# q's opening in six pieces of x, matmul passes of 320, 256 and 288 columns, and each product's last chunk finished tile by tile

## The chip, the cores and the metric

The kernel runs on one core of a Trainium2 chip. The metric is the device time of one execution in microseconds (us), as the median of several runs. Times inside an execution come from one profiled execution, counted from the start of its span.

## The reference

One layer of a decoder is computed in float32 for 256 prompt rows and 32 sample rows (8 sequences of 4), so T = 288 rows of D = 2048. Cut to what matters here:

```
h = rms_norm(x, g_pre);  z = h @ w_in            # -> q | k | v | u | v_g, 1024 columns each
A = block-sparse attention(q, k, v, paged cache) # 8 heads of 128, rotary on q and k
B = gelu(u) * spatial_gating(layer_norm(gelu(v_g)))
mix = (sigmoid(h @ Wg_a) * (A @ Wa) + sigmoid(h @ Wg_b) * (B @ Wb)) @ w_o
x = x + rms_norm(mix)
x = x + rms_norm(SwiGLU(rms_norm(x)))            # FFN_HIDDEN = 5632
x = x + (p @ w_ple) * sigmoid(rms_norm(x) @ w_ple_gate)
```

## The kernel before

Activations lie transposed, features on the 128 partitions and the T rows along the free dimension; `x` is 16 slabs of 128 features (`KD = 16`). Each large product is a call of `product(w, c0, ks, ...)`, which makes 256 output columns as two PSUM tiles (t = 0 and 1) of 128 columns each. It walks the contraction in chunks of four slabs. For a chunk it loads 512 KB of weights on SyncE's queue (tile `wr`, four buffers), ScalarE rounds them to the high part (`wh`, L224), VectorE takes the rest (`wl`, L225). For each slab and tile TensorE then makes three passes, called a triplet below:

```
nc.tensor.matmul(accs[t], wh[:, i, c], x[:, :T + wide], start=k == 0, stop=False)               # L228
nc.tensor.matmul(accs[t][:, wide:T], wh[:, i, c], x[:, T + wide:], start=False, stop=False)     # L229
late["mm"] = nc.tensor.matmul(accs[t][:, :T], wl[:, i, c], x[:, :T], start=False, stop=k == n - 1)  # L230
```

`x` holds the high part of the activations in columns 0 to 287 and the low part in 288 to 575. With `wide=0` the passes have 288, 288 and 288 columns. With `wide=32`, which only the product with `w_ffn_out` (tile `f`) used, they have 320, 256 and 288: the first pass also takes 32 columns of the low part, into 32 more columns of PSUM. At the product's end ScalarE copies these out (`rest`, L234) and VectorE adds them back (L235), before `done` reads the tile.

The tiles of a product come from PSUM pools: up to the end of the attention `acc` has three banks, `aux` three and `long` two; after it `acc` has six. There is one order of instructions for each engine, set by a scheduler at build time; `tc.issue_after` ties a step behind another in that order.

q has four products of 256 columns. In the opening two of them (`q2`) go together: for each of four pieces of x (four slabs, 576 KB) come `h_parts` (L189 on ScalarE, L190 on VectorE: high and low part of x times its gain), one chunk of either product, the load of the next piece and the squares for the norm `r0`. The other two products follow, each product's result goes through `rope`, then k, v and the rest, with the pages of the cache (`kt`, `vt`, 512 KB each, three buffers of four pages) loaded and multiplied in between (`page_load`, L560, on SyncE's queue too). Constants (`cst`, `kcst`) come by GpSimd's queue, `cm` by ScalarE's. Ten warm-up matmuls (`wake`) run while the first loads are on their way.

The last stage multiplies with `w_ple_gate` (tile `pg`); `pg_done` makes two output tiles of each product and writes both in one transfer.

Of the kernel before, what the change touches and what calls it, by code (L numbers as in the profile page):

```python
# [41 lines left out]
QUADS = NPG // 4  # L42
WAKE, WR, BIG, PT, AUX, PB, LEAD, EG, LE, N1, N2, REST = 10, 4, 3, 1, 3, 2, 6, 2, 4, 20, 38, 325.0

# [64 lines left out]
def tile_hybrid_step(ctx: ExitStack, tc: tile.TileContext, a: dict, o: list):  # L109
# [25 lines left out]

    def x_load(c):
        nc.sync.dma_start(xs[c], a["x"][:, c * XK:c * XK + XK])
# [4 lines left out]
    x_load(0)  # L142
    cst = perm.tile([128, 128], F32, name="cst")
    nc.gpsimd.dma_start(cst, a["c_perm"][:, :128])
    ident = cst
# [8 lines left out]
    kcst = p_kv.tile([128, C_PERM - 128], F32, name="kcst")  # L154
    nc.gpsimd.dma_start(kcst, a["c_perm"][:, 128:])

# [28 lines left out]

    def h_parts(c):
        for i in range(XK):
            k = c * XK + i
            nc.scalar.activation(hh[:, k], xs[c][:, i], AF.Copy, scale=g_pre[:, k:k + 1])  # L189
            nc.vector.scalar_tensor_tensor(hl[:, k], xs[c][:, i], g_pre[:, k:k + 1], hh[:, k], op0=ALU.mult, op1=ALU.subtract)  # L190

# [8 lines left out]
    def r0_of():  # L200
# [5 lines left out]
        rstd_of(r0, r0p, p_x0.tile([128, T], F32, name="r0t"))  # L206


    def product(w, c0, ks, part, done, name, of="acc", wide=0, hold=()):


        accs = [bank([128, T + wide], f"{name}{t}", of) for t in range(2)]
        n = len(ks)
        for k0 in range(0, n, 4):
            m = min(4, n - k0)
            raw = perm.tile([128, 4, GC], F32, name="wr", bufs=WR)
            r0 = ks[k0] * 128
            nc.sync.dma_start(raw[:, :m], w[r0:r0 + m * 128, c0:c0 + GC].rearrange("(k p) c -> p k c", p=128))
# [28 lines left out]

    def q_gen(g, of="acc"):
        yield from product(w_in, g * GC, K16, hpart, lambda x: rope(qT[:, 2 * g:2 * g + 2], x), "q", of)
# [12 lines left out]
    p_a, end_a = pool("p_a", "right")  # L262
    cm = p_a.tile([128, C_MIX], F32, name="cm")
    nc.scalar.dma_start(cm, a["c_mix"])

# [506 lines left out]

    for q in q2 + [q_gen(2), q_gen(3)]:
        drain(q)
# [187 lines left out]
    for half in range(2):  # L962
# [41 lines left out]
        for g in range(8):  # L1004
            if half and g == 6:
                le_weights(range(LE, 8))
            drain(product(w_fo, g * GC, ks, lambda k: dhl[:, k], lambda x, g=g: fo_done(x, g), "f", wide=32))

# [5 lines left out]
    def pg_done(x, g):  # L1014
        for t in range(2):
            m = 2 * g + t
            gt = p_f.tile([128, T], F32, name="pgt", tag="fs", bufs=4)
            nc.vector.tensor_tensor(gt, x[t], r3, ALU.mult)
            nc.scalar.activation(gt, gt, AF.Sigmoid)
            nc.vector.tensor_tensor(gt, gt, le[:, m], ALU.mult)  # L1020
            nc.vector.tensor_tensor(x1[:, m], x1[:, m], gt, ALU.add)
        nc.sync.dma_start(y_o[:, 2 * g:2 * g + 2], x1[:, 2 * g:2 * g + 2])

# [57 lines left out]
```

## Time and profile before

| | us |
|---|---|
| median of 3 runs | 1820.64 (1820.21 to 1822.02) |
| the profiled execution | 1820.68 |
| its span, first to last instruction | 1818.9 |
| outside the span | 1.8 |
| TensorE busy | 1798.5 (99% of the span) |
| VectorE busy | 951.9 (52%) |
| ScalarE busy | 769.2 (42%) |

The profiled execution stands 0.04 us from the median, so its times can be set against it as they are. A busy share of TensorE is no measure of its pace: matmuls overlap, and a row's duration is longer than the distance from one start to the next. The pace of a stretch is its length over the number of matmuls that start in it.

### The profile page before, as it was taken

Reading aid. Unit: us, or ns where it says so; the run is one execution under the profiler, and the core shown is the slowest. Engines: PE = TensorE matmul, PEld = TensorE weight load, DVE = VectorE, ACT = ScalarE, POOL = GpSimd, SP = SyncE. Lnnn points to the kernel's source line nnn. Section 1 sums busy time; section 2 is a strip of 40 time slices with the busy share of each in tenths; the row PEclk is TensorE's granted clock in tenths of the full one; section 3 lists DMA queues with packets and bytes.
Section 4 is the critical chain, followed back from the end, with each engine's and each line's share of the span. In section 5 each row is a group of like instructions: output and inputs, shape, how many; then the busy total and the mean of one; then the engine's idle time right before and its main releaser. Section 6 shows DMA issues by size and latency. Waiting matters only on the chain.

```text
span 1818.9 us, 38387 instructions
## 1 busy us (share of the span) xinstructions
PE 1798.5 (99%) x15818; PEld 1752.1 (96%) x15818; DVE 951.9 (52%) x1363; ACT 769.2 (42%) x1081; POOL 90.6 (5%) x169
## 2 busy tenths in 40 slices
PE   7999999999999999999999999999999999999998
PEld 7999899999999989999999999999999999999998
DVE  6654447544344346544854555434455554444774
ACT  5334465444333344445533333333333333444642
POOL 1010112000000000011000000000000000011000
PEclk9999999999999999999999999999999999999999
DMA  9589999999999995555555555455555555546363
GB/s 345 163 280 367 323 360 337 365 350 359 352 345 368 358 321 201 170 164 161 152 169 166 163 167 169 157 168 165 172 165 172 163 164 170 165 158 195 122 196 112
DMA packets 309136, 414.81 MB, mean 228 GB/s; under 512 B 13120, under 2 KB 273344, under 8 KB 308832
## 3 DMA queue, kind: packets, MB, share of 16 engines
q1 hardware_dynamic: 307728, 409.16, 67.0%
q8 instruction: 124, 2.03, 0.5%
q0 software_dynamic: 944, 2.79, 0.4%
q10 hardware_dynamic: 288, 0.41, 0.1%
q14 instruction: 52, 0.43, 0.1%
HBM read 407.45 MB, written 4.85 MB: 227 GB/s over the span
## 4 chain that ended last, share of the span: by engine, by line
PE 94%; DVE 3%; DMA 1%; SPq 1%; issue 1%; ACT 1%; DVEq 0%; ACTq 0%
PE f L228 6%; PE f L230 5%; PE fg L228 5%; PE fg L230 5%; PE fg L229 5%; PE fa L230 5%; PE fa L228 5%; PE fa L229 5%; PE f L229 5%; PE values L696 3%; PE scores L598 3%; PE gb L228 2%; PE ga L228 2%; PE gb L230 2%; PE o L228 2%; PE o L230 2%
## 5 line engine op out<-in xcount | busy, mean ns | idle before, releaser
L225 DVE TENSOR_TENSOR wl<-wr,wh 128x1024 fp32r<-128x1024 f32 x512 | 618.8, 1209 | 708.2 <-ACT wh L224 704.4
L224 ACT CAST wh<-wr 128x1024 fp32r<-128x1024 f32 x512 | 530.9, 1038 | 881.0 <-PE f L229 140.4
L228 PE MATMUL f<-dhl,wh 128*128 128x320 f32 x704 | 217.1, 308 | 0.0
L229 PE MATMUL fg<-zhl,wh 128*128 128x288 f32 x704 | 208.2, 296 | 0.0
L230 PE MATMUL fa<-zhl,wl 128*128 128x288 f32 x704 | 206.8, 295 | 1.2 <-DVE wl L225 1.2
L229 PE MATMUL fa<-zhl,wh 128*128 128x288 f32 x704 | 207.9, 296 | 0.0
L228 PE MATMUL fg<-zhl,wh 128*128 128x288 f32 x704 | 207.3, 295 | 0.2 <-ACT wh L224 0.2
L230 PE MATMUL fg<-zhl,wl 128*128 128x288 f32 x704 | 207.0, 295 | 0.0
L230 PE MATMUL f<-dhl,wl 128*128 128x288 f32 x704 | 207.0, 294 | 0.0
L228 PE MATMUL fa<-zhl,wh 128*128 128x288 f32 x704 | 206.3, 296 | 0.1
L229 PE MATMUL f<-dhl,wh 128*128 128x256 f32 x704 | 196.6, 279 | 0.0
L230 PEld LDWEIGHTS fa<-zhl,wl 128*128 128x128 f32 x704 | 133.3, 189 | 1.4 <-DVE wl L225 1.4
L230 PEld LDWEIGHTS fg<-zhl,wl 128*128 128x128 f32 x704 | 133.3, 190 | 0.0
L229 PEld LDWEIGHTS f<-dhl,wh 128*128 128x128 f32 x704 | 132.4, 188 | 0.0
L228 PEld LDWEIGHTS fg<-zhl,wh 128*128 128x128 f32 x704 | 132.1, 188 | 0.4 <-ACT wh L224 0.4
L229 PEld LDWEIGHTS fa<-zhl,wh 128*128 128x128 f32 x704 | 132.4, 188 | 0.1
L229 PEld LDWEIGHTS fg<-zhl,wh 128*128 128x128 f32 x704 | 132.3, 188 | 0.0
L228 PEld LDWEIGHTS fa<-zhl,wh 128*128 128x128 f32 x704 | 131.6, 188 | 0.7 <-ACT zhl L937 0.4
L230 PEld LDWEIGHTS f<-dhl,wl 128*128 128x128 f32 x704 | 132.2, 188 | 0.0
L228 PEld LDWEIGHTS f<-dhl,wh 128*128 128x128 f32 x704 | 132.0, 188 | 0.0
L228 PE MATMUL gb<-hhl,wh 128*128 128x288 f32 x256 | 76.7, 300 | 0.0
L228 PE MATMUL ga<-hhl,wh 128*128 128x288 f32 x256 | 76.5, 299 | 0.0
(327 smaller groups left out, 3740.6 us busy)
## 6 DMA issues: line engine op xcount, KB each, us to landing
wr<-in_w_ffn_in SPq DMA_DIRECT2D x176, 512.0 KB, 3.7
kt<-in_cache_k SPq DMA_DIRECT2D x128, 512.0 KB, 7.7
vt<-in_cache_v SPq DMA_DIRECT2D x128, 512.0 KB, 6.6
wr<-in_w_in SPq DMA_DIRECT2D x80, 512.0 KB, 7.2
wr<-in_w_ffn_out SPq DMA_DIRECT2D x80, 512.0 KB, 3.4
wr<-in_w_gate SPq DMA_DIRECT2D x64, 512.0 KB, 7.4
wr<-in_w_o SPq DMA_DIRECT2D x32, 512.0 KB, 3.5
wr<-in_w_ple_gate SPq DMA_DIRECT2D x32, 512.0 KB, 3.5
```

The lines of the kernel that those rows point to most:

```text
L224: nc.scalar.copy(wh[:, :m], raw[:, :m])
L225: nc.vector.tensor_tensor(wl[:, :m], raw[:, :m], wh[:, :m], ALU.subtract)
L228: nc.tensor.matmul(accs[t], wh[:, i, c], x[:, :T + wide], start=k == 0, stop=False)
L229: nc.tensor.matmul(accs[t][:, wide:T], wh[:, i, c], x[:, T + wide:], start=False, stop=False)
L230: late["mm"] = nc.tensor.matmul(accs[t][:, :T], wl[:, i, c], x[:, :T], start=False, stop=k == n - 1)
L598: i = nc.tensor.matmul(sp[b][32 * g:32 * g + 32, 4 * n:4 * n + 4], Q[:, h2, g, dq], kt[:, :, c:c + 32], start=h2 == 1 and dq == 0, stop=h2 ...
L696: i = nc.tensor.matmul(oa[b][32 * g:32 * g + 8], w[:, n, 32 * g + 8 * part:32 * g + 8 * part + 8], v[:, :, g], start=first and part == 3, ...
```

## The change

It does five things. All products get `wide=32`. q's opening takes three products together instead of two (tiles from `acc`, `long` and `aux`), and takes x in six pieces of 1, 1, 2, 4, 4 and 4 slabs, with weight chunks of the same size (small ones in tiles `w1` and `w2`). The constants and `cm` go to SyncE's queue behind certain weight loads, and the first twelve cache pages are each tied behind a weight load, from the tenth on. In a product's last chunk all slabs of tile 0 come before those of tile 1. The very last output tile is finished in two halves of 144 columns, and the last product writes each of its output tiles by itself. The warm-up has eight matmuls instead of ten.

```diff
+    pieces = [(0, 1), (1, 2), (2, 4)] + [(k, k + XK) for k in range(XK, KD, XK)]
+    def x_load(k0, k1):
+        (nc.scalar if k0 == 1 else nc.sync).dma_start(xs[k0 // XK][:, k0 % XK:k0 % XK + k1 - k0], a["x"][:, k0:k1])
...
-    def product(w, c0, ks, part, done, name, of="acc", wide=0, hold=()):
+    def product(w, c0, ks, part, done, name, of="acc", wide=32, cuts=None, hold=()):
         accs = [bank([128, T + wide], f"{name}{t}", of) for t in range(2)]
         n = len(ks)
-        for k0 in range(0, n, 4):
-            m = min(4, n - k0)
-            raw = perm.tile([128, 4, GC], F32, name="wr", bufs=WR)
+        for k0, k1 in cuts or [(k, min(k + 4, n)) for k in range(0, n, 4)]:
+            m = k1 - k0
+            if cuts and m < 4:
+                raw = p_x0.tile([128, m, GC], F32, name=f"w{m}", bufs=6 // m)
+            else:
+                raw = perm.tile([128, 4, GC], F32, name="wr", bufs=WR)
...
-            for i, t in [(i, t) for i in range(m) for t in range(2)] if m == 4 else [(i, t) for t in range(2) for i in range(m)]:
+            steps = [(i, t) for i in range(m) for t in range(2)]
+            for i, t in sorted(steps, key=lambda s: s[1]) if k1 == n else steps:
...
-    q2 = [q_gen(0), q_gen(1, "long")]
-    for c in range(KD // XK):
-        h_parts(c)
-        for q in q2:
+    q3 = [q_gen(g, of, pieces) for g, of in enumerate(("acc", "long", "aux"))]
+    for i, (k0, k1) in enumerate(pieces):
+        h_parts(k0, k1)
+        for q in q3:
+            if k1 == KD and q is q3[2]:
+                squares(k1 // XK - 1)
+                with tc.issue_after(late["mm"].ins):
+                    r0_of()
             next(q)
-        if c + 1 < KD // XK:
-            x_load(c + 1)
-        squares(c)
-    r0_of()
+        if 1 < i + 1 < len(pieces):
+            x_load(*pieces[i + 1])
+        if k1 % XK == 0 and k1 < KD:
+            squares(k1 // XK - 1)
+    with tc.issue_after(loads[11].ins):
+        nc.sync.dma_start(cst, a["c_perm"][:, :128])
+        nc.sync.dma_start(kcst, a["c_perm"][:, 128:])
...
+            if len(issued) < FIRST:
+                st.enter_context(tc.issue_after(loads[9 + len(issued)].ins))
...
+            for c in (slice(0, T // 2), slice(T // 2, T)) if m == KD - 1 else (slice(0, T),):
+                nc.vector.tensor_tensor(gt[:, c], x[t][:, c], r3[:, c], ALU.mult)
+                nc.scalar.activation(gt[:, c], gt[:, c], AF.Sigmoid)
+                nc.vector.tensor_tensor(gt[:, c], gt[:, c], le[:, m, c], ALU.mult)
+                nc.vector.tensor_tensor(x1[:, m, c], x1[:, m, c], gt[:, c], ALU.add)
```

What the scheduler makes of it is seen at three places. The first is the start of SyncE's queue, where all weights, x and pages are issued (`x_76` to `x_79` are x's four tiles of four slabs). Before:

```order
L137 DMA x_76<-in_x 128x1152
L218 DMA wr<-in_w_in 128x4x256 x2
L137 DMA x_77<-in_x 128x1152
L218 DMA wr<-in_w_in 128x4x256 x2
L137 DMA x_78<-in_x 128x1152
L137 DMA x_79<-in_x 128x1152
L559 TENSOR_LOAD pt_sb
```

There the first page follows these rows, ahead of the fifth weight load. The same queue of the changed kernel:

```order
L139 DMA x_76<-in_x 128x288
L225 DMA w_109<-in_w_in 128x256
L225 DMA w_123<-in_w_in 128x256
L225 DMA w_137<-in_w_in 128x256
...
L139 DMA x_76<-in_x 128x576
...
L139 DMA x_77<-in_x 128x1152
L225 DMA wr<-in_w_in 128x4x256 x3
L139 DMA x_78<-in_x 128x1152
L225 DMA wr<-in_w_in 128x4x256
L139 DMA x_79<-in_x 128x1152
L273 DMA cst<-in_c_perm 128x128
L274 DMA kcst<-in_c_perm 128x448
```

One slab of x and small weight chunks now come first, and all of x, the two constants and thirteen weight loads stand ahead of the first page. Behind these rows come four pages, and then one weight load and one page in turn.

The second place is VectorE at the end of the fourth product with k (tiles `k_1334` and `k_1335` before, `k_1412` and `k_1413` after), in the stretch in which `acc` has three banks. Before:

```order
L225 TENSOR_TENSOR wl<-wr,wh 128x1024 x3
L631 TENSOR_REDUCE gpage<-P_1531 128x16
L633 TENSOR_REDUCE gate<-gpage 128x8
L278 TENSOR_TENSOR kT<-k_1334,r_107 128x288
L278 TENSOR_TENSOR kT<-k_1335,r_107 128x288
```

After:

```order
L649 TENSOR_REDUCE gpage<-P_1609 128x16
L651 TENSOR_REDUCE gate<-gpage 128x8
L243 TENSOR_TENSOR k_1412<-k_1412,rest 128x32
L294 TENSOR_TENSOR kT<-k_1412,r_104 128x288
L232 TENSOR_TENSOR wl<-wr,wh 128x1024
L243 TENSOR_TENSOR k_1413<-k_1413,rest 128x32
L294 TENSOR_TENSOR kT<-k_1413,r_104 128x288
```

Each tile now has its add of the 32 columns directly ahead of its read, and a chunk's `wl` stands between the two tiles.

The third place is the end of TensorE's order (the last product with `w_ple_gate`, tiles `pg_22755` and `pg_22756`). Before, the triplets of the two tiles alternate to the end; after:

```order
L236 MATMUL pg_22755<-zhl,wh 128x320
L237 MATMUL pg_22755<-zhl,wh 128x256
L238 MATMUL pg_22755<-zhl,wl 128x288
L236 MATMUL pg_22756<-zhl,wh 128x320
L237 MATMUL pg_22756<-zhl,wh 128x256
L238 MATMUL pg_22756<-zhl,wl 128x288
L236 MATMUL pg_22756<-zhl,wh 128x320
```

Tile 0 has its last triplet four triplets ahead of the product's end, and the widths of the three passes are seen in the rows.

## Rows read from the trace of the kernel before

**Rows 1.** The page's head: span, and busy time of each engine.

```profile
span 1818.9 us, 38387 instructions
PE 1798.5 (99%) x15818; PEld 1752.1 (96%) x15818; DVE 951.9 (52%) x1363; ACT 769.2 (42%) x1081; POOL 90.6 (5%) x169
```

**Rows 2.** Waits of TensorE, whole span: total us, times, longest us.

```profile
PE q L228 <- ACT wh L224: 6.3, 2, 3.8
PE q L230 <- DVE wl L225: 2.5, 3, 1.6
PE pg L230 <- DVE wl L225: 1.2, 1, 1.2
PE fa L230 <- DVE wl L225: 1.2, 1, 1.2
...
PE values L696 <- DMA vt<-in_cache_v: 0.6, 1, 0.6
```

**Rows 3.** Windows of the opening: length, busy us (count) by engine, PEclk, DMA share, GB/s.

```profile
1.00:9.54 8.54, 4.64 (x21) 4.34 (x21) 2.18 (x8) 4.39 (x8) 5.49 (x12) 1.00 0.93 298
9.54:12.98 3.44, 3.44 (x13) 3.16 (x14) 2.61 (x3) 3.44 (x6) 0.00 (x0) 0.50 1.05 363
12.98:43.13 30.15, 26.60 (x188) 25.29 (x187) 24.25 (x39) 14.80 (x21) 0.00 (x0) 1.00 1.05 385
43.13:50.50 7.37, 5.79 (x26) 5.56 (x25) 4.76 (x6) 2.45 (x3) 0.00 (x0) 0.54 0.63 191
50.50:72.47 21.97, 21.97 (x167) 21.97 (x167) 12.38 (x15) 6.84 (x7) 0.00 (x0) 1.00 0.54 163
```

**Rows 4.** Timeline up to q's first matmul: start, us, instruction, idle before it.

```profile
5.52 1.81 ACT L189 ACTIVATE hhl<-x,gains 128x288 fp32r<-128x288 f32 x4 [2.83 <-DMA gains<-in_gains]
...
8.44 1.05 ACT L224 CAST wh<-wr 128x1024 fp32r<-128x1024 f32 x1 [1.11 <-DMA wr<-in_w_in]
...
9.54 0.61 PE L228 MATMUL q<-hhl,wh 128*128 128x288 f32 x1 [3.84 <-ACT wh L224]
```

**Rows 5.** DMA issues: count, KB each, median us from issue to landing.

```profile
wr<-in_w_ffn_out SPq DMA_DIRECT2D x16, 256.0 KB, 2.6
...
gains<-in_gains ACTq DMA_DIRECT2D x1, 44.0 KB, 4.7
```

**Rows 6.** Groups by line and form: count, busy us, mean ns of one, idle before.

```profile
L225 DVE TENSOR_TENSOR wl<-wr,wh 128x1024 fp32r<-128x1024 f32 x496 | 607.7, 1226 | 685.7 <-ACT wh L224 681.9 <-DMA kt<-in_cache_k 3.2 <-PE values L696 0.2
L224 ACT CAST wh<-wr 128x1024 fp32r<-128x1024 f32 x496 | 520.9, 1051 | 849.5 <-PE fg L229 136.5 <-PE fa L229 127.6 <-PE f L229 108.8
...
L190 DVE SCALAR_TENSOR_TENSOR hhl<-x,gains,hhl 128x288 fp32r<-128x288 f32 x16 | 7.1, 515 | 0.0
...
L1018 DVE TENSOR_TENSOR pgt<-pg,r_x 128x288 f32<-128x288 f32 x16 | 6.6, 455 | 9.3 <-PE pg L230 9.3
...
L235 DVE TENSOR_TENSOR f<-f,rest 128x32 f32<-128x32 f32 x32 | 6.2, 193 | 2.1 <-ACT rest L234 2.0
...
L281 DVE TENSOR_TENSOR rope<-rope,cm 32x576 f32<-32x576 f32 x8 | 5.9, 742 | 0.1
...
L234 ACT COPY rest<-f 128x32 f32<-128x32 f32 x32 | 5.6, 175 | 3.6 <-PE f L230 3.6
```

**Rows 7.** Groups by line, 0 to 72.5 us: the norm's matmuls.

```profile
L205 PE MATMUL r0p<-x,ones_d 128*128 128x288 f32 x4 | 1.1, 406 | 0.0
```

**Rows 8.** Windows with matmuls of product alone: o; fa and fg; f.

```profile
750.00:849.00 99.00, 99.00 (x751) 99.00 (x750) 41.58 (x38) 45.70 (x65) 14.92 (x13) 1.00 0.56 180
890.00:1140.00 250.00, 250.00 (x1887) 250.00 (x1887) 130.44 (x166) 98.25 (x122) 0.00 (x0) 1.00 0.54 167
1142.00:1278.00 136.00, 136.00 (x1034) 136.00 (x1033) 55.62 (x63) 51.75 (x77) 0.00 (x0) 1.00 0.52 165
```

**Rows 9.** Timeline of the end, from the last matmul.

```profile
1812.99 0.29 PE L230 MATMUL pg<-zhl,wl 128*128 128x288 f32 x1
...
1814.67 0.82 DVE L1021 TENSOR_TENSOR x<-x,pgt 128x288 f32<-128x288 f32 x2
```

More of the change, by code (lines that the diff above doesn't have):

```diff
@@ L42 @@
 QUADS = NPG // 4
-WAKE, WR, BIG, PT, AUX, PB, LEAD, EG, LE, N1, N2, REST = 10, 4, 3, 1, 3, 2, 6, 2, 4, 20, 38, 325.0
+WAKE, FIRST, WR, BIG, PT, AUX, PB, LEAD, EG, LE, N1, N2, REST = 8, 12, 4, 3, 1, 3, 2, 6, 2, 4, 20, 38, 325.0
 C_ID, C_G, C_OWN, C_L = 0, 128, 256, 256 + TS * NB
@@ L134, in tile_hybrid_step @@
     xs = [p_x0.tile([128, XK, T], F32, name=f"x{c}") for c in range(KD // XK)]
-    def x_load(c):
-        nc.sync.dma_start(xs[c], a["x"][:, c * XK:c * XK + XK])
+    pieces = [(0, 1), (1, 2), (2, 4)] + [(k, k + XK) for k in range(XK, KD, XK)]
+    def x_load(k0, k1):
+        (nc.scalar if k0 == 1 else nc.sync).dma_start(xs[k0 // XK][:, k0 % XK:k0 % XK + k1 - k0], a["x"][:, k0:k1])
     gains = perm.tile([128, 88], F32, name="gains")
@@ L141, in tile_hybrid_step @@
     g_pre, g_pm, g_pf, g_pof, g_pl, g_vn = (gains[:, 16 * i:min(16 * i + 16, 88)] for i in range(6))
-    x_load(0)
+    x_load(*pieces[0])
+    x_load(*pieces[1])
     cst = perm.tile([128, 128], F32, name="cst")
-    nc.gpsimd.dma_start(cst, a["c_perm"][:, :128])
     ident = cst
@@ L154, in tile_hybrid_step @@
     kcst = p_kv.tile([128, C_PERM - 128], F32, name="kcst")
-    nc.gpsimd.dma_start(kcst, a["c_perm"][:, 128:])
     ones_d = perm.tile([128, 128], F32, name="ones_d")
@@ L184, in tile_hybrid_step, with h_parts @@
     hh, hl = hhl[:, :, :T], hhl[:, :, T:]
[L186 to L190, printed above, removed]
+    def h_parts(k0, k1):
+        for k in range(k0, k1):
+            x = xs[k // XK][:, k % XK]
+            nc.scalar.activation(hh[:, k], x, AF.Copy, scale=g_pre[:, k:k + 1])
+            nc.vector.scalar_tensor_tensor(hl[:, k], x, g_pre[:, k:k + 1], hh[:, k], op0=ALU.mult, op1=ALU.subtract)
     def squares(c):
@@ L206, in r0_of @@
         rstd_of(r0, r0p, p_x0.tile([128, T], F32, name="r0t"))
-    def product(w, c0, ks, part, done, name, of="acc", wide=0, hold=()):
+    loads = []
+    def product(w, c0, ks, part, done, name, of="acc", wide=32, cuts=None, hold=()):
         accs = [bank([128, T + wide], f"{name}{t}", of) for t in range(2)]
         n = len(ks)
-        for k0 in range(0, n, 4):
-            m = min(4, n - k0)
-            raw = perm.tile([128, 4, GC], F32, name="wr", bufs=WR)
+        for k0, k1 in cuts or [(k, min(k + 4, n)) for k in range(0, n, 4)]:
[4 more added lines that the diff above has]
+                raw = perm.tile([128, 4, GC], F32, name="wr", bufs=WR)
             r0 = ks[k0] * 128
-            nc.sync.dma_start(raw[:, :m], w[r0:r0 + m * 128, c0:c0 + GC].rearrange("(k p) c -> p k c", p=128))
+            loads.append(nc.sync.dma_start(raw[:, :m], w[r0:r0 + m * 128, c0:c0 + GC].rearrange("(k p) c -> p k c", p=128)))
             wh = perm.tile([128, 4, GC], F32R, name="wh", bufs=3)
@@ L245, in tile_hybrid_step, with q_gen @@
     w_gate = a["w_gate"].rearrange("l k c -> (l k) c")
-    def q_gen(g, of="acc"):
-        yield from product(w_in, g * GC, K16, hpart, lambda x: rope(qT[:, 2 * g:2 * g + 2], x), "q", of)
-    q2 = [q_gen(0), q_gen(1, "long")]
-    for c in range(KD // XK):
-        h_parts(c)
-        for q in q2:
-            next(q)
-        if c + 1 < KD // XK:
-            x_load(c + 1)
-        squares(c)
-    r0_of()
+    def q_gen(g, of="acc", cuts=None):
+        yield from product(w_in, g * GC, K16, hpart, lambda x: rope(qT[:, 2 * g:2 * g + 2], x), "q", of, cuts=cuts)
+    q3 = [q_gen(g, of, pieces) for g, of in enumerate(("acc", "long", "aux"))]
[6 more added lines that the diff above has]
+                    r0_of()
+            next(q)
+        if 1 < i + 1 < len(pieces):
[5 more added lines that the diff above has]
+        nc.sync.dma_start(kcst, a["c_perm"][:, 128:])
     end_x0.close()
@@ L263, in tile_hybrid_step @@
     cm = p_a.tile([128, C_MIX], F32, name="cm")
-    nc.scalar.dma_start(cm, a["c_mix"])
+    with tc.issue_after(loads[13].ins):
+        nc.sync.dma_start(cm, a["c_mix"])
     A = p_h.tile([128, H, T], F32, name="A")
@@ L771, in cache_gen @@
         products()
-    for q in q2 + [q_gen(2), q_gen(3)]:
+    for q in q3 + [q_gen(3)]:
         drain(q)
@@ L1006, in tile_hybrid_step @@
                 le_weights(range(LE, 8))
-            drain(product(w_fo, g * GC, ks, lambda k: dhl[:, k], lambda x, g=g: fo_done(x, g), "f", wide=32))
+            drain(product(w_fo, g * GC, ks, lambda k: dhl[:, k], lambda x, g=g: fo_done(x, g), "f"))
     r4 = norm_gap("fo", range(LE, 8))
@@ L1017, in pg_done @@
             gt = p_f.tile([128, T], F32, name="pgt", tag="fs", bufs=4)
[L1018 to L1022, printed above, removed]
+            for c in (slice(0, T // 2), slice(T // 2, T)) if m == KD - 1 else (slice(0, T),):
[3 more added lines that the diff above has]
+                nc.vector.tensor_tensor(x1[:, m, c], x1[:, m, c], gt[:, c], ALU.add)
+            if g == 7:
+                nc.sync.dma_start(y_o[:, m], x1[:, m])
+        if g < 7:
+            nc.sync.dma_start(y_o[:, 2 * g:2 * g + 2], x1[:, 2 * g:2 * g + 2])
     pg = [product(w_pg, g * GC, K16, zpart, lambda x, g=g: pg_done(x, g), "pg",
```

## The prediction

> **What bounds the kernel now.** I read the page's head first: TensorE is busy for 1798.5 of 1818.9 us [rows 1], so only two things can move the time much: the stretches where it waits, and its pace while it runs. The waits came next. In the whole span only 12 us of wait show, and 8.8 of them stand before matmuls of q; its waits for cache pages come to 0.6 us [rows 2]. So the opening needs its own windows [rows 3], and the middle of the kernel is bound by the number of matmuls times their pace, read from windows that hold nothing but matmuls of `product` [rows 8].
>
> q begins at 9.54 us [rows 4] and ends at 72.47, where the last window of the opening is cut. That is 62.9 us for 4 products of 32 triplets. At full speed they would need less: product o made about 749 matmuls in 99 us (two of the 751 only reach into the window), 0.1322 us each, 0.397 us a triplet [rows 8]; 128 x 0.397 = 50.8, and the four matmul rows of the norm `r0` take at most 1.1 [rows 7]. So 11 us are lost behind 9.54. A part is clock: the granted clock was 0.50, the lower of its two levels (1.2 of 2.4 GHz), from 9.54 to 12.98, after TensorE had stood idle for over 3 us, and averages 0.54 from 43.13 to 50.50, after another stretch with idle time [rows 3]. Half speed costs half of each, 1.7 and about 3. The rest are waits for weights: 8.8 less the 3.8 ahead of the first matmul [rows 2] is 5.0, and shorter ones. DMA moved 385 GB/s from 12.98 to 43.13 [rows 3], so the lanes were full; the pages in SyncE's order stood ahead of weights that q was waiting for.
>
> **The change part by part.**
>
> *The start.* Before, ScalarE waits for the gains until 5.52, makes four high parts (1.81), waits 1.11 for 512 KB of weights and rounds them (1.05), then TensorE starts [rows 4]. After, q's first matmul needs the gains (44 KB), one slab of x (144 KB), one weight chunk of 128 KB, one high part on ScalarE (1.81 / 4, say 0.5), its low part on VectorE (0.515 [rows 6], beside the rounding), since the first pass now reads 32 columns of it, and a small rounding. That one is new: between the copy of 32 columns (0.175) and the cast of 1024 (1.05) [rows 6] a straight line gives 0.37 for 256. When do the pieces land? A transfer of 256 KB takes 2.6 us from issue to landing when little else moves; the gains took 4.7 beside 576 KB of x [rows 5]. Issued near 0.8 and 1.2, they land between 3.8 and 5.5; I take 4.1, nearer the first, as there is a quarter of the x beside them. 4.1 + 0.5 + 0.4 = 5.0. Ends: 4.7 and 6.4. The warm-up's 20 rows made nearly all of the 4.64 us busy ahead of q [rows 3]; 16 of them end near 1.0 + 3.7 = 4.7. So the idle time that stood ahead of the half clock is gone, and I count no half clock.
>
> *The opening's supply.* I add up SyncE's new order in KB. Ahead of the fourteenth weight load's end stand gains 44, x 2304, nine small weight chunks 1536, five of 512, constants 288 and four pages of 512: 8780 KB, 8.99 MB. At the rates of rows 3 (298 GB/s to 9.54, 363 to 12.98, 385 behind it) it lands at 26.5, and with the cast at 27.5. TensorE wants it after 56 triplets of 0.3955: 5.0 + 22.1 = 27.1. Four loads and four pages later (4.19 MB, 10.9 us) the eighteenth lands at 37.4, cast 38.5, wanted at 39.8 plus what was lost. So supply and demand meet, with 0.4 us of wait at one place, and each further pair of load and page (1.05 MB, 2.7 us) is faster than a chunk (3.16 us). *VectorE behind it:* three products finish together, near 45 us, and their six reads (0.45 each) and three ropes (four steps of about 0.74 each) are 11.6 us, with a `wl` of 1.23 every 3.16 us beside them [rows 6]. That fills VectorE for some 19 us, and what may be late is the `wl` of q's fourth product and of k's first: I take 1 us of wait, at most 3. Sum: 5.0 + 128 x 0.3955 + 1.1 + 0.4 + 1.0 = **58.1**, against 72.47: **-14.4**. Ends: 4.7 and no wait, 56.4 (-16.1); a start at 6.4, 3 us for VectorE, 3 us for supply at a rate 15% lower and one more half-clock stretch like the first (1.7), 66 (-6.5).
>
> *Pages later.* They land some 10 us later. But in TensorE's order the first scores stand behind 607 matmuls of `product`, some 80 us at 0.132, and DMA ran at only 163 GB/s from 50.50 on [rows 3]: 0. If that cover were gone, each late page would cost its 1.4 us.
>
> *The passes.* The three widths sum to 864 columns either way. In windows of fa and fg (288 each) I count 1885 starts in 250 us, 0.1326 us each; in f, which had 320, 256 and 288 already, 1032 in 136 us, 0.1318; o, with 288, 0.1322 [rows 8]. So a matmul is 0.4 to 0.8 ns shorter with the unequal widths. fa and fg have 44 products of 32 triplets, 4224 matmuls, x 0.8 = 3.2; the others (q, k, v, g, u, gb, ga, b, a, o, pg: 1920 triplets, 5760 matmuls) x 0.4 = 2.1. **-5.3**. Ends: 0 if f is quicker for another reason (its operand lies elsewhere); and as o and fa differ by 0.4 ns at equal widths, an operand can move the pace by as much in either direction, so +4 and -9.
>
> The Trainium skill (TensorE: Matmul & The Clock Gate, Back-to-back issue gap) gives the warm gap as columns over 2.4 GHz plus a constant 2.5 ns, which makes the three passes 367.5 ns in either split; by it this part would be 0 and the sum 1806.3. The trace's triplets are 395 to 398 ns and not equal, so it does not settle this; it is why the second case below has a good chance.
>
> *The rest columns.* Each product now has two copies on ScalarE (0.175) and two adds on VectorE (0.193) [rows 6]. 112 products are new to it: 39 and 43 us of work on engines with 1050 and 867 us free [rows 1]. On the path they stand only where a tile's bank is wanted soon: up to the attention's end `acc` has three banks, and a product's second tile takes the bank of the last product's tile 0. That tile now ends four triplets before the product's end (1.58 us), and the bank is wanted two matmuls (0.26) into the next: 1.84 us of cover for 0.175 + 0.193 + 0.455 = 0.82. So 0; the tile order pays for the widths. With the triplets in turn the cover would be 0.40 + 0.26 = 0.66, and 0.16 us late in each of 44 products, 7 us.
>
> *First passes that read the low part.* Behind the two norms TensorE starts fa and pg on high parts alone; now it waits about 0.5 us more for a low part, twice. But 1.2 us of wait for a `wl` stand some 10 us further on in both places [rows 2], set by VectorE, so a later start eats these: 0, at most +1.
>
> *The end.* Before, from the last matmul's end (1813.28) to the last add's (1815.49) it is 2.2 us [rows 9]. After: copy 0.18, add 0.19, then two halves. From 0.193 for 32 columns and 0.455 for 288 a straight line gives 0.30 for 144; with three VectorE steps and a sigmoid in two halves the last add ends some 2.4 us behind the matmul. The last transfer is half as big. 0, within 0.3.
>
> **Sum.** 1820.68 - 14.4 - 5.3 = 1801.0, and the profiled execution stands at the median: **1801**.
>
> **The rivals.** *The widths give nothing:* the opening alone, 1806. For it: equal columns, and o nearly as fast as f at equal widths. *The opening gives half:* supply falls behind because four pages stand ahead of the fourteenth load and one ahead of each later one, or the early pieces land late; about -7, 1808.5. For it: my margin at that load is -0.4 us, and small pieces are priced from few rows. *Given back later:* pages come too late once TensorE is earlier. Against it stand the 0.6 us of page waits [rows 2]; all but the widths lost, 1815. *Slower:* in the 44 products with three banks the copy waits behind a cast (1.05) and the add behind a `wl` (1.23) [rows 6]; then the chain is 3.1 us instead of 0.82, 1.26 past its cover, and 44 x 1.26 = 55 us: 1856. It decides from a chain of 2.3 us on (0.45 x 44 = 20). Against it: in VectorE's order the add and the read stand together with no `wl` between, and before f's copies ScalarE was the one that waited (3.6 us in all, for the matmul [rows 6]).
>
> **How the numbers follow.** Forecast 0.56; widths nothing 0.20; opening half 0.15; given back 0.04; slower 0.05. The forecast's own range is 1797 to 1805. With the next two cases and the bounds the range is **1795 to 1811**. A change of 0.2%, 3.6 us, is about what a measurement of this kernel can tell from none. Faster by more: 0.94; within: 0.02; slower: 0.04.
>
> **What would show it.** Right: q's first matmul near 5 us and k's near 58; granted clock 1.00 through the opening; TensorE's waits at q below 3 us; windows of fa and fg at 0.1318 us a matmul; no new wait of TensorE between 100 and 700 us. Wrong: a wait of q's passes for weights near 28 us; a half clock; fa at 0.1326 still; gaps at the second tile of products in the three-bank stretch.

## The result and the profile after

The changed kernel takes **1801.01 us** (median of 5 runs, 1799.85 to 1803.19) against 1820.3 for the kernel before (1818.87 to 1822.02): a ratio of 0.9896, 95% interval 0.9882 to 0.9911. The forecast was 1801. That the total was hit is luck: the opening gave less than forecast, the passes and some parts priced at nothing gave more, and the errors cancel.

The profiled execution is the longest of the five (1803.19 us). In the changed kernel's rows the three passes are lines 236 to 238, the rounding is 231, `wl` 232, the copy and the add of the 32 columns 242 and 243. The page's head and TensorE's waits, as in [rows 1, 2]:

```profile
span 1801.4 us, 38858 instructions
...
PE 1784.3 (99%) x15814; PEld 1739.3 (97%) x15814; DVE 985.3 (55%) x1596; ACT 799.8 (44%) x1312; POOL 80.8 (4%) x167
```

```profile
PE q L236 <- ACT wh L231: 2.2, 2, 1.7
PE pg L236 <- DVE zhl L956: 1.5, 1, 1.5
PE fa L236 <- DVE zhl L956: 1.5, 1, 1.5
PE pg L238 <- DVE wl L232: 1.3, 1, 1.3
PE fa L238 <- DVE wl L232: 1.3, 1, 1.3
PE values L714 <- DMA vt<-in_cache_v: 1.2, 1, 1.2
...
PE q L238 <- DVE wl L232: 0.9, 2, 0.5
```

q's waits fell from 8.8 to 3.1 us. Ahead of the first pass of fa and of pg TensorE now waits 1.5 us for a low part (line 956). At fa this is new; at pg it takes the place of a wait for a high part in the kernel before:

```profile
PE pg L228 <- ACT zhl L937: 0.9, 1, 0.9
```

The waits for `wl` behind them are about as long as before (1.3 against 1.2). The windows of the opening, cut at q's first matmul, at two waits, at a change of clock and at k's first matmul (columns as in [rows 3]):

```profile
1.00:4.88 3.88, 3.78 (x16) 3.49 (x16) 0.56 (x4) 2.47 (x5) 3.46 (x5) 1.00 0.70 198
4.88:15.09 10.21, 10.14 (x71) 9.83 (x72) 7.29 (x16) 8.02 (x17) 0.90 (x7) 1.00 0.99 328
15.09:29.26 14.17, 13.20 (x98) 12.75 (x97) 13.56 (x18) 10.62 (x15) 0.00 (x0) 1.00 1.05 388
29.26:32.75 3.49, 1.32 (x8) 0.87 (x7) 1.23 (x1) 1.04 (x1) 0.00 (x0) 1.00 1.07 374
32.75:36.16 3.41, 3.41 (x16) 3.41 (x16) 1.23 (x1) 1.51 (x2) 0.00 (x0) 0.50 1.07 375
36.16:63.23 27.07, 27.07 (x202) 26.86 (x202) 18.94 (x34) 10.29 (x17) 0.00 (x0) 1.00 0.89 297
```

q starts at 4.88 us and k at 63.23 (before: 9.54 and 72.47). From 29.26 on TensorE is busy for only 1.32 of 3.49 us; then the granted clock is 0.50 for 3.41 us. SyncE's queue and ScalarE's timeline there tell why (start, duration, instruction, idle time before it):

```profile
15.73 3.87 SPq L578 DMA_DIRECT2D kt<-in_cache_k  x4
21.27 0.39 SPq L225 DMA_DIRECT2D wr<-in_w_in  x1
...
21.30 1.05 ACT L231 CAST wh<-wr 128x1024 fp32r<-128x1024 f32 x1 [0.43 <-DMA wr<-in_w_in]
...
30.16 1.04 ACT L231 CAST wh<-wr 128x1024 fp32r<-128x1024 f32 x1 [3.29 <-DMA wr<-in_w_in]
32.95 1.05 ACT L231 CAST wh<-wr 128x1024 fp32r<-128x1024 f32 x1 [1.74 <-DMA wr<-in_w_in]
```

The load issued at 21.27 is the fourteenth; four pages were issued ahead of it. Its cast starts at 30.16, for which ScalarE had been idle for 3.29 us. The cast at 21.30 is that of the thirteenth load, which has no page ahead of it.

The pace, in windows with product's matmuls alone: o; fa and fg; f (as in [rows 8]).

```profile
740.00:839.00 99.00, 99.00 (x753) 99.00 (x752) 43.38 (x54) 48.83 (x83) 11.08 (x13) 1.00 0.56 179
880.00:1120.00 240.00, 240.00 (x1833) 240.00 (x1832) 133.27 (x205) 100.77 (x160) 0.00 (x0) 1.00 0.55 168
1130.00:1266.00 136.00, 136.00 (x1034) 136.00 (x1033) 54.86 (x64) 51.99 (x76) 0.00 (x0) 1.00 0.52 165
```

With two matmuls taken off each count, as the prediction did, fa and fg take 240/1831 = 0.1311 us a matmul (before 0.1326, forecast 0.1318), o 0.1318 (0.1322), and f, whose form did not change, 0.1318 as before.

Behind the last matmul the sum's "2.4 us" to the last add is 1798.53 - 1796.07 = 2.46:

```profile
1795.78 0.29 PE L238 MATMUL pg<-zhl,wl 128*128 128x288 f32 x1
...
1798.01 0.52 DVE L1040 TENSOR_TENSOR x<-x,pgt 128x144 f32<-128x144 f32 x2
```

The span cut by the first matmul of each product, in us (the last column but one is an experiment that sets the widths back, the last one with later pages; both below):

| stretch | before | after | widths_undone | pages_later |
|---|---|---|---|---|
| up to q | 9.54 | 4.88 | 4.50 | 4.69 |
| q to k | 62.93 | 58.35 | 57.20 | 53.88 |
| k to g | 137.37 | 137.05 | 137.40 | 136.98 |
| g to b (attention) | 289.36 | 290.07 | 288.90 | 290.80 |
| b to o (b, ga, a) | 248.86 | 246.66 | 248.33 | 246.66 |
| o to fa, with the norm | 109.68 | 110.70 | 109.64 | 110.70 |
| fa to pg, with the second norm | 850.59 | 844.64 | 849.86 | 844.55 |
| pg to the end | 110.57 | 109.05 | 109.86 | 108.94 |

So 9.2 us came from the time up to k's first matmul and 8.3 from behind it, in the profiled executions. By the medians the kernel gained 1.8 us more, as the profiled execution is the longest of its five; where the shorter ones gained this, no profile shows. The opening is the likely place: widths_undone and tile_order_undone below have the same opening and reach k at 61.71 and 60.81, both without a half clock.

### The profile page after: what moved, and what is told of

Read it like the earlier page. It is cut to its first block, busy times and chain, and to the rows that moved or that the text cites. A ratio compares the mean times of both kernels' runs of the same rounds, so it can differ in the third digit from the quotient of the medians.

```text
span 1801.4 us, 38858 instructions
## 1 busy us (share of the span) xinstructions
PE 1784.3 (99%) x15814; PEld 1739.3 (97%) x15814; DVE 985.3 (55%) x1596; ACT 799.8 (44%) x1312; POOL 80.8 (4%) x167
## 4 chain that ended last, share of the span: by engine, by line
PE 96%; DVE 1%; DMA 1%; ACT 0%; SPq 0%; issue 0%; DVEq 0%; ACTq 0%
PE fa L236 6%; PE fg L236 6%; PE f L236 6%; PE f L238 5%; PE fa L238 5%; PE fg L238 5%; PE f L237 5%; PE fa L237 5%; PE fg L237 5%; PE values L714 3%; PE scores L616 3%; PE ga L236 2%; PE o L236 2%; PE pg L236 2%; PE gb L236 2%; PE ga L238 2%
## 5 line engine op out<-in xcount | busy, mean ns | idle before, releaser
L232 DVE TENSOR_TENSOR wl<-wr,wh 128x1024 fp32r<-128x1024 f32 (+1 forms) x509 | 614.7, 1209 | 702.9 <-ACT wh L231 699.3
L231 ACT CAST wh<-wr 128x1024 fp32r<-128x1024 f32 (+1 forms) x509 | 526.3, 1035 | 745.1 <-issue 178.2
L236 PE MATMUL fa<-zhl,wh 128*128 128x320 f32 x704 | 218.8, 311 | 1.5 <-DVE zhl L956 1.5
L236 PE MATMUL fg<-zhl,wh 128*128 128x320 f32 x704 | 218.9, 311 | 0.0
L237 PE MATMUL fa<-zhl,wh 128*128 128x256 f32 x704 | 196.6, 279 | 0.0
L237 PE MATMUL fg<-zhl,wh 128*128 128x256 f32 x704 | 196.4, 279 | 0.0
L236 PE MATMUL pg<-zhl,wh 128*128 128x320 f32 x256 | 79.3, 312 | 1.5 <-DVE zhl L956 1.5
L236 PE MATMUL gb<-hhl,wh 128*128 128x320 f32 x256 | 79.9, 314 | 0.4 <-DVE eg L411 0.4
```

## The experiments

Each kernel was timed in five rounds beside the kernel before, which stood at 1819.6 to 1820.3 us; ratios are to it. Two theories were tested first: *the four pages* ahead of the fourteenth load cost the opening 4 us, and *the widths* carry nearly all of the gain behind q. Their rivals were a debt left by the early, slow transfers, and the order of the last chunk as the cause of the gain.

**pages_later: the first pages six loads later**

```diff
-                st.enter_context(tc.issue_after(loads[9 + len(issued)].ins))
+                st.enter_context(tc.issue_after(loads[15 + len(issued)].ins))
```

> The changed kernel with the first twelve cache pages tied six weight loads later (the 16th to 27th load in place of the 10th to 21st); nothing else is changed. Theory A: the wait of 1.86 + 0.63 us near 29 to 32.5 us and the half clock behind it come from four pages that land ahead of the 14th weight load; here that load lands near 26, there is no wait over 1 us between 18 and 60 us, the granted clock stays 1.00, q's products end 3.5 to 4.5 us sooner and the time is about 1797. Rival B: the load is late since the early pieces were moved at 200 to 290 GB/s and the queues carry the debt, pages or not: the wait stays and so does 1801. Rival C: the opening gains the 4 us but the attention waits for its pages, and the time is again 1801 or more.

Measured: 1798.83 us (1798.24 to 1799.36), ratio 0.9878 (0.9863 to 0.9893). The same windows of its opening, and ScalarE's casts of the fourteenth load (24.64) and the next two:

```profile
29.26:32.75 3.49, 3.49 (x28) 3.49 (x28) 2.58 (x3) 1.38 (x2) 0.00 (x0) 1.00 1.03 356
32.75:36.16 3.41, 3.41 (x28) 3.41 (x27) 1.23 (x1) 0.76 (x2) 0.00 (x0) 1.00 1.05 373
36.16:58.57 22.41, 22.41 (x168) 22.20 (x167) 15.78 (x31) 8.65 (x15) 0.00 (x0) 1.00 0.99 338
```

```profile
24.64 1.04 ACT L231 CAST wh<-wr 128x1024 fp32r<-128x1024 f32 x1
...
26.65 1.03 ACT L231 CAST wh<-wr 128x1024 fp32r<-128x1024 f32 x1
29.14 1.05 ACT L231 CAST wh<-wr 128x1024 fp32r<-128x1024 f32 x1 [1.47 <-PE q L237]
```

There is no wait at this place, no half clock, and the later cast waits for TensorE instead of for a load. Without the four pages ahead of it the fourteenth load is cast 5.5 us sooner; 2.10 MB at 388 GB/s are 5.4. So the pages were the cause, and rival B falls. k starts at 58.57, near the 58.1 of the prediction. Of 4.7 us gained there, 0.7 go again in the attention, where the wait for a cache tile is 1.9 us (by the medians 2.2 us are gained):

```profile
PE values L714 <- DMA vt<-in_cache_v: 1.9, 1, 1.9
```

**pages_mid: three loads later**

```diff
-                st.enter_context(tc.issue_after(loads[9 + len(issued)].ins))
+                st.enter_context(tc.issue_after(loads[12 + len(issued)].ins))
```

> The changed kernel with the first twelve cache pages tied three weight loads later (13th to 24th), half of what pages_later does (six later: 1798.8 us, the 1.86 us wait near 29 us and the half clock gone, k's products from 58.46 us, but 1.9 us of wait for a cache tile in the attention where the changed kernel has 1.2). Theory A: the four pages still land behind the 14th load, so the opening keeps its gain, k's products start at 58.5, and the attention's wait is shorter: 1798 to 1799. Rival B: half of the pages stand ahead of a weight load again, a wait of 1 to 2 us comes back between 26 and 40 us, and the time is 1800 to 1801.

Measured: 1797.75 us (1797.67 to 1799.12), 0.9879 (0.9863 to 0.9894), the lowest median of all. k starts at 59.32, between the two, the attention's wait is 1.2 us: theory A. All its runs lie below the changed kernel's shortest (1799.85), but the two were not timed side by side, and the intervals of the ratios overlap.

**opening_undone: the opening of before, the rest as changed** (two of the lines, against the changed kernel)

```diff
-    q3 = [q_gen(g, of, pieces) for g, of in enumerate(("acc", "long", "aux"))]
+    q2 = [q_gen(0), q_gen(1, "long")]
...
-    for q in q3 + [q_gen(3)]:
+    for q in q2 + [q_gen(2), q_gen(3)]:
```

> The changed kernel with the opening of before (x in four pieces, two of q's products in step, the constants on GpSimd's and ScalarE's queues, pages not tied to the weight loads); the passes, the last chunk's order and the end stay as changed. Theory A: the opening is worth what the two traces show at the start of k's products, 72.47 less 63.23, so the time comes to 1801.0 + 9.2 = about 1810. Theory B, the prediction's sum: 14.4 us, about 1815, if half of what the opening gains were given back somewhere behind it in the changed kernel. Rival C: what the opening gains is given back later by late pages, and the time stays within 3 us of 1801.

Measured: 1812.00 us (1810.44 to 1812.57), 0.9950 (0.9937 to 0.9964), k from 72.50. The opening is worth 11.0 us by the medians, between theories A and B, and 9.3 by k's start in the two profiles; rival C falls.

**four_pieces: pages_later with x and the first weights in four pieces, three products in step**

```diff
-    pieces = [(0, 1), (1, 2), (2, 4)] + [(k, k + XK) for k in range(XK, KD, XK)]
+    pieces = [(k, k + XK) for k in range(0, KD, XK)]
```

> pages_later (1798.83 us) with x and the first weights again in four pieces of four chunks; three of q's products still go in step, and the pages and constants stay tied to the same loads. It tells the two halves of the new opening apart. Theory A, the early start is what the small pieces bring and all of it is kept: q's first matmul comes at 9 to 10 us in place of 4.6, k's products start 4 to 5 us later than 58.5, and the time is about 1803. Theory B, the opening is held by the supply of x and weights, of which the same bytes have to land: TensorE starts later but waits less behind it, k's products start within 1.5 us of 58.5, and the time is 1799 to 1800.

Measured: 1801.74 us (1800.83 to 1805.35), 0.9904 (0.9887 to 0.9920), 2.9 us over pages_later: between the two theories, nearer A. q starts at 8.12 us, after 3.4 us without a matmul, at half clock:

```profile
1.00:8.12 7.12, 3.63 (x16) 3.45 (x17) 1.85 (x7) 4.28 (x8) 4.35 (x10) 0.98 0.92 284
8.12:11.50 3.38, 3.38 (x13) 3.10 (x14) 2.60 (x3) 3.33 (x4) 0.00 (x0) 0.54 1.07 378
11.50:58.90 47.40, 47.40 (x357) 47.19 (x356) 35.96 (x56) 24.22 (x37) 0.00 (x0) 1.00 0.96 325
```

k's first matmul comes only 0.3 us later than in pages_later, but that mark misleads here, as k's product starts before the last one of q has ended; v's comes 3.0 later (121.64 against 118.65). So the small pieces bring 3 us, and three products in step, with the pages and constants tied behind weight loads (the pages six loads later than in the changed kernel), bring the greater part: from opening_undone to four_pieces v's first matmul goes from 132.50 to 121.64. No run tells the step of three and the tied loads apart.

**widths_undone: 288, 288, 288 again, in all but ffn_out**

```diff
-    def product(w, c0, ks, part, done, name, of="acc", wide=32, cuts=None, hold=()):
+    def product(w, c0, ks, part, done, name, of="acc", wide=0, cuts=None, hold=()):
...
```

> The changed kernel (median 1801.0 us) with passes of 288, 288 and 288 columns again in every product but ffn_out's; the opening, the order of a product's last chunk and the last output tile stay as changed. Theory A, read from the two traces: the widths carry nearly all of the 8.3 us that the kernel gained behind q's products, so this one loses 7 to 9 us and comes to about 1809, with fa and fg back from 393.4 to about 397.8 ns a triplet and f, whose form is the same in all, at 395.6. Theory B, the prediction's own sum: 5.3 us, about 1806. Rival C: the width is worth nothing and the gain behind q came from the order of the last chunk, so the time stays at 1801 and fa's triplets at 393 to 394 ns.

Measured: 1807.92 us (1806.76 to 1809.95), 0.9930 (0.9917 to 0.9944): 6.9 us, just under theory A's 7 to 9 and above B's 5.3; as the ratio's interval is some 2.5 us either way, the medians alone don't exclude B. The pace decides: fa and fg take 240/1810 = 0.1326 us again:

```profile
880.00:1120.00 240.00, 240.00 (x1812) 240.00 (x1812) 125.75 (x163) 96.33 (x119) 0.00 (x0) 1.00 0.54 165
```

From start to start a triplet of fa is 397.2 ns here and 393.4 in the changed kernel (about 670 undisturbed ones each). By the table the widths save 5.2 us from fa to pg, 0.8 behind it, 1.7 in b, ga and a, and cost 1.06 at the first norm. Without the norm that is 7.7 us.

**tile_order_undone: the last chunk's tiles in turn**

```diff
-            for i, t in sorted(steps, key=lambda s: s[1]) if k1 == n else steps:
+            for i, t in sorted(steps, key=lambda s: s[1]) if m < 4 and not cuts else steps:
```

> The changed kernel with the tiles of the last chunk of each 16-chunk product in turn again, as before the change. The prediction said that the three-bank stretch would then wait 0.16 us for the rest columns in each of 44 products, 7 us, which gives 1808. Rival: the copy and the add are hidden all the same, or the scheduler places the triplets so that the second tile ends late in both, and the time stays at 1801 within 0.7 us.

Measured: 1799.38 us (1798.80 to 1800.18), 0.9881 (0.9866 to 0.9896): not 1808. Behind k this profile is 0.6 us shorter than that of the changed kernel. ga, whole (first ga to first a; after, then this one):

```profile
553.88:686.38 132.50, 132.50 (x1432) 121.34 (x1431) 63.04 (x106) 54.10 (x81) 0.95 (x4) 1.00 0.91 323
```

```profile
549.56:683.04 133.48, 132.96 (x1432) 121.38 (x1431) 63.37 (x106) 53.87 (x81) 0.95 (x4) 1.00 0.91 323
```

1.0 us here, half of it a wait for a `wl`, and 0.4 from pg on is all that the order is worth. The trace shows why it isn't 7: the scheduler doesn't keep the triplets in turn as written. The two tiles of a product still end 1.0 us apart (its first copies of `rest` in ga start at 569.66 and 570.67), and no matmul waits for a bank. So the order that the prediction priced was not run. That the time is shorter all the same comes, in the profiles, from the opening (k from 60.81, no half clock) and the attention (1.7 us shorter).

**wide16 and wide48: pages_later with 304, 272 and 336, 240 columns**

```diff
-    def product(w, c0, ks, part, done, name, of="acc", wide=32, cuts=None, hold=()):
+    def product(w, c0, ks, part, done, name, of="acc", wide=16, cuts=None, hold=()):
```

> pages_later (1798.8 us) with passes of 304, 272 and 288 columns in the 16-chunk products (ffn_out's stay at 320, 256, 288). Where 288, 288, 288 became 320, 256, 288 a triplet of ffn_in fell from 397.2 to 393.4 ns and the stretch from the first ffn_in product to the end by 6.05 us. Theory A: the gain goes with the difference of the widths, so half of it is lost: 395.3 ns a triplet, about +3 us, 1802. Theory B: what counts is only that the wide pass covers the load of the next weights, or that the passes differ at all: 393.4 ns and 1799. Theory C: a pass of 272 columns is no faster a column than one of 288 and only 256 is, since its length is a whole number of some step: 397 ns and 1805.

> pages_later (1798.8 us) with passes of 336, 240 and 288 columns in every product, ffn_out's too. Theory A (the gain goes with the difference): 391.5 ns a triplet in ffn_in, 3 us less there and 2 us less in the others, about 1794. Theory B (it is only that they differ): no change, 1799. Theory C (256 is what counts): 397 ns, 1805 or more. A fourth way: the shorter pass no longer covers a weight load, and the triplets get longer than 400 ns.

In both kernels ffn_out had the new widths too, other than the expectation of wide16 says. Measured: 1812.03 us (1811.08 to 1812.88), 0.9956 (0.9942 to 0.9970), and 1811.32 us (1810.94 to 1811.68), 0.9954 (0.9940 to 0.9967): 13.2 and 12.5 us slower than pages_later. Windows of fa and fg, then of f, in wide16:

```profile
880.00:1120.00 240.00, 240.00 (x1812) 240.00 (x1811) 130.26 (x201) 98.73 (x157) 0.00 (x0) 1.00 0.54 166
1140.00:1276.00 136.00, 136.00 (x1022) 136.00 (x1022) 54.60 (x63) 52.21 (x79) 0.00 (x0) 1.00 0.52 167
```

f, at 0.1318 us with 320 and 256, is at 136/1020 = 0.1333 in both. Theory A falls (there is no trend with the difference of the widths), and so does B (not any two unequal widths do it). Theory C's 397 ns fit fa (397.8 and 396.8 ns), but both times lie 6 us or more above its 1805; f is slower too. 320 and 256 is the fastest of the four splits tried in fa, and of the three tried in f.

**starts_moved: where a pass begins, on pages_mid**

```diff
-    ahl = p_ab.tile([128, H, 2 * T], F32R, name="ahl")
+    ahl = p_ab.tile([128, H, 2 * T + 64], F32R, name="ahl")
...
-            yield from product(w_a, g * GC, K8, lambda k: ahl[:, k], done, "a")
+            yield from product(w_a, g * GC, K8, lambda k: ahl[:, k], done, "a", wide=0, low=T + 32)
...
-    zhl = p_z.tile([128, KD, 2 * T], F32R, name="zhl")
+    zhl = p_z.tile([128, 32 + KD * 2 * T], F32R, name="zhl")[:, 32:].rearrange("p (k c) -> p k c", k=KD)
```

> pages_mid (1797.75 us) with two changes of where the moving rows start, in two stages. In a_out (a) the passes are 288, 288, 288 columns again, but the low part begins 320 columns into the row, not 288, so that the second pass begins at a whole number of 64 columns, as it does with 320 and 256. In ffn_in and ple_gate (fa, fg, pg) the widths stay 320, 256, 288, and the whole array begins 32 columns later in its buffer. So far 304/272 and 336/240 columns gave 397.7 and 396.7 ns a triplet in fa where 320/256 gave 393.3, and 288/288 gave 397.2; a gave 395.6 with 320/256 and 400.0 with 288/288. Theory A, the columns of the pass count (256 and 320 are multiples of 64): a goes back to 400.0 ns, fa stays at 393.3, and the time is about 0.6 us longer. Theory B, the address at which a pass starts counts: a keeps 395.6 ns with 288 columns, and fa goes to 396 ns or more, which costs 1664 triplets by 3 to 4 ns = 5 to 7 us.

Measured: 1798.92 us (1797.52 to 1799.32), 0.9880 (0.9863 to 0.9896). Only the edit in a moved anything. `zhl` comes from a pool that grows down from the far end of the on-chip memory: the 32 columns put ahead of it moved its start down by as much, and in the built programs its rows begin at the same byte (141536) in pages_mid and here. So fa's 393.4 ns, the same in both, say nothing about starts. A triplet of a, over all 127 that can be measured:

| a: columns, start of the low part | ns a triplet |
|---|---|
| 288, 288 at 288 (widths_undone) | 400.0 |
| 304, 272 at 304 (wide16) | 399.9 |
| 288, 288 at 320 (this one) | 396.7 |
| 336, 240 at 336 (wide48) | 395.6 |
| 320, 256 at 320 (after) | 395.6 |

At equal widths the low part's start at 320, with rows of 640 columns instead of 576, takes 3.3 of the 4.4 ns. So theory A falls: the pass's length isn't what counts first. Theory B's forecast for a nearly holds, and its forecast for fa was not tested. But 336 is as good as 320 in a and not in fa (396.8). What rule the engine follows stays open.

**narrow_after_norm: 288 columns in the products behind the norms, on pages_later**

```diff
-            pairs += [product(w_fi, c0, K16, zpart, done_a, "fa", hold=hold), product(w_fi, FF + c0, K16, zpart, done_g, "fg")]
+            pairs += [product(w_fi, c0, K16, zpart, done_a, "fa", hold=hold, wide=0 if half == 0 and g < 2 else 32),
+                      product(w_fi, FF + c0, K16, zpart, done_g, "fg", wide=0 if half == 0 and g < 1 else 32)]
...
-    pg = [product(w_pg, g * GC, K16, zpart, lambda x, g=g: pg_done(x, g), "pg",
+    pg = [product(w_pg, g * GC, K16, zpart, lambda x, g=g: pg_done(x, g), "pg", wide=0 if g < 3 else 32,
```

> pages_later (1798.8 us) with passes of 288 columns again in the three products in step behind each of the two norms (six products of ffn_in and ple_gate). Their first pass of 320 columns reads 32 columns of the low part, for which the trace shows TensorE waiting 1.5 us at each norm, where the kernel with 288 columns everywhere waits 0.9 at one of them and not at the other. Theory A: the wait is what the width costs there, 1.06 us at the first norm and 0.6 at the second by the lengths of those stretches, less 192 triplets at 3.9 ns = 0.75 us that the narrow passes lose: 0.9 us gained, about 1798. Rival: TensorE then waits as long for the low part one pass later, and only the 0.75 us is lost: 1799.5.

Measured: 1798.09 us (1797.28 to 1798.42), 0.9879 (0.9864 to 0.9894). The first pass now waits 0.9 us, for a high part:

```profile
PE fa L236 <- ACT zhl L955: 0.9, 1, 0.9
PE pg L236 <- ACT zhl L955: 0.9, 1, 0.9
```

By stretches it gains 0.56 us from o to fa, and loses it from fa to pg (+0.21) and behind pg's first matmul (+0.84): 0.5 lost. The lower median goes with a shorter wait for a cache tile in the profile, 0.9 us and not 1.9. The rival, which had 0.75 lost, was nearer.

**halves_undone: the last tile whole, on pages_later**

```diff
-            for c in (slice(0, T // 2), slice(T // 2, T)) if m == KD - 1 else (slice(0, T),):
-                nc.vector.tensor_tensor(gt[:, c], x[t][:, c], r3[:, c], ALU.mult)
+            nc.vector.tensor_tensor(gt, x[t], r3, ALU.mult)
...
-            if g == 7:
-                nc.sync.dma_start(y_o[:, m], x1[:, m])
-        if g < 7:
-            nc.sync.dma_start(y_o[:, 2 * g:2 * g + 2], x1[:, 2 * g:2 * g + 2])
+        nc.sync.dma_start(y_o[:, 2 * g:2 * g + 2], x1[:, 2 * g:2 * g + 2])
```

> pages_later (1798.83 us) with the last output tile whole again and both tiles of the last product written by one transfer. The prediction put the halves at nothing within 0.3 us: the stretch from ple_gate's first matmul to the end, 106.13 us in pages_later, should be 106.1 to 106.5 long here and the time 1798.8 to 1799.2. Rival: the halves save one of the four steps behind the last matmul (the four on a whole tile take some 1.5 us), 0.7 us, so this comes to 1799.6.

Measured: 1798.31 us (1797.75 to 1799.91), 0.9881 (0.9865 to 0.9898): the medians don't tell the two apart. From pg's first matmul to the span's end it is 109.63 us, where pages_later, pages_mid and four others with the halves have 108.94 to 109.09. (The 106.13 of the expectation ran to the last add; by that measure it is 106.38.) So the halves are worth 0.6 us, 0.3 of it in the chain and the rest behind the last add, where the last transfer is smaller: nearer to the rival's 0.7 than to nothing. The attention of this run shows no wait for a cache tile at all, which hides them.

**combined: pages_mid and narrow_after_norm**

> pages_mid (1797.75 us) and narrow_after_norm in one kernel: the pages three weight loads later, and passes of 288 columns in the three products in step behind each norm. If the two add, as they touch stages 800 us apart, the 0.74 us by which narrow_after_norm was below pages_later comes off pages_mid: 1797.0 us, with the stretch from w_o's first matmul to ffn_in's at 110.1 us in place of 110.7. Rival: the difference of 0.74 us was mostly the attention's wait for a cache tile, 0.9 us in that kernel's profile and 1.9 in that of pages_later, and nothing comes off: 1797.5 to 1798.

Measured: 1799.49 us (1798.25 to 1800.65), 0.9883 (0.9866 to 0.9899): no better than either part. Its profile shows a new half clock behind the second norm, after waits of 0.9 and 1.2 us some 12 us apart, with 0.1 between (first from pg's first matmul, then from the end of the last wait):

```profile
1687.60:1700.34 12.74, 11.36 (x80) 10.69 (x80) 12.74 (x23) 9.70 (x17) 0.00 (x0) 1.00 0.04 13
1700.34:1705.00 4.66, 4.66 (x23) 4.66 (x24) 4.66 (x7) 2.10 (x5) 0.00 (x0) 0.63 0.66 208
```

narrow_after_norm has the same matmuls and waits there, no half clock, and 1.5 us less from pg to the end. pages_mid has the lowest median, but the kernels with later pages lie too close together for their intervals to rank them.

## Why the prediction came out, step by step

- **The start:** 5.0 forecast, 4.88 measured; right, and no half clock followed it.
- **The opening's supply** is the step that failed. "It lands at 26.5" was 30.1, and "0.4 us of wait" became a hole of 3.5 us with 1.3 us of work in it, and half of 3.4 us lost to the clock behind it; 1.0 us of waits went before it, from 15.09 to 29.26. These come to 4.9 us where the sum had 1.4 for all waits, so they explain 3.5 of the 5.1 us by which k came later than 58.1; part of the rest is the pace from 4.88 to 15.09, 71 matmuls in 10.21 us, 0.144 each. By the windows, what came in up to 30.1 us is 0.77 + 3.35 + 5.50 + 0.31 = 9.9 MB, 0.9 MB more than the sum counted ahead of this load. At 388 GB/s the 0.9 MB are 2.4 us; the other 1.2 are the slow start, 198 GB/s up to 4.88 us where I took 298. The 0.9 MB are not peculiar to this load: the sum up to the thirteenth, with no page ahead of it, is 5.5 MB, and by its cast at 21.30 some 6.5 had come in. The term that the sum left out is the time between a load's bytes and its landing, and [rows 5] had it: 256 KB took 2.6 us from issue to landing, of which the bytes at 385 GB/s are 0.7. Whether later loads share the lanes meanwhile or the landing itself takes so long, no view here separates. The four pages were in the sum; that without them the load is there in time is shown by pages_later. The rival "opening gives half" named this very mechanism; its size was between: 9.2 to 11 us in place of 14.4 or 7.
- **VectorE behind it:** 1 us of wait forecast, none seen from 36.16 to 63.23.
- **Pages later:** 0 forecast. The cache-tile wait went from 0.6 [rows 2] to 1.2 us; pages_later and halves_undone, alike up to the last product, show 1.9 and none. So it differs between executions and hides effects of half a microsecond.
- **The passes** were mis-sized the other way: -5.3 forecast, 6.9 measured by setting the widths back, with the norms' loss in it; without that loss the stretches of the table give 7.7. The step that failed took f's pace for that of all products with these widths. fa went past it: 0.1311 us a matmul and not 0.1318, a gain of 3.8 ns a triplet where the sum had 2.4. The lower end that I named, an operand's own pace, is what happened.
- The Trainium skill (TensorE: Matmul & The Clock Gate, Back-to-back issue gap) gives a matmul by itself a gap of its columns over 2.4 GHz plus a constant; by it widths that sum to 864 cost the same. The trace, a stream of weight loads and matmuls, disagrees: 393.4, 396.8, 397.2 and 397.8 ns in fa for four splits of the same 864 columns. The measurement decides, and the rival "widths give nothing" falls.
- **The rest columns:** 0 was right, but the reason, that the new order saves 7 us, is not shown: with the order set back the tiles still end 1.0 us apart, not 0.40. In tile_order_undone the add even stands behind a `wl` once (the copy at 570.67 in ga, its add at 571.95), which is the mechanism of the rival "slower", and still no matmul waits for a bank.
- **First passes that read the low part:** 0, "at most +1", failed: the later `wl` waits did not eat the new ones. o to fa is 1.02 us longer, and at pg the wait grew from 0.9 to 1.5, so the upper end was passed too.
- **The end:** 0 within 0.3; from the last matmul's start to the span's end it is 5.62 against 5.91 us before. The halves are worth 0.6 by their own run, so the copy and the add took back about half of that.
- **Behind k the sum of the rest** is 8.3 us: the widths give 5.8 in the profiles, and 2.4 came without them (before to widths_undone). By their own runs tile order and halves are worth some 2 of these; the attention's wait for a cache tile, 0.6 us in one profile and none in the other, would make up for the rest.

## What to carry over

A load lands later than the bytes up to its end over the rate say, here by some 2 us, so price that too, and keep what isn't needed yet out of the queue until the tight load has landed: moving the pages down SyncE's order was worth 2 to 3 us by the medians. A pace measured on one operand doesn't price another: price a split of columns by running it on the product in question. Before a kernel that should move an array is read, see that the array did move. When parts of a sum cancel, only a cut of the span by stage shows it, and a profile's own waits (here one for a cache tile) have to be taken off before medians half a microsecond apart are read.

## What the runs showed of the hardware

- 864 columns in three fp32r passes cost 387 to 404 ns. The time differs with the split, with the low part's place in the row, and from product to product; single triplets come in a few values (in f nearly all are 390, 393, 394, 403 or 404 ns).
- The half clock can follow holes shorter than those before the change, but need not. It came once behind 3.5 us with 1.3 us of matmuls in them, once behind waits of 0.9 and 1.2 us. In widths_undone a hole as deep at the same place was followed by full clock, in tile_order_undone a wait of 0.95 and one of 0.46 us, in narrow_after_norm the waits of combined. The rows of widths_undone:

```profile
29.26:32.75 3.49, 1.10 (x6) 0.87 (x7) 1.38 (x2) 1.04 (x1) 0.00 (x0) 1.00 1.07 375
32.75:36.16 3.41, 3.41 (x28) 3.41 (x27) 1.23 (x1) 1.58 (x2) 0.00 (x0) 1.00 1.08 377
```
